# Taking 32 frames of the fifth dense tile out of the dense expert stage and gathering their expert rows instead

## The chip, the cores and the metric

The kernel runs on one core of one Trainium2 chip. The metric is the device time of one execution in microseconds (us), the median of three runs. The core has five engines that run their own instruction streams in order: TensorE (PE, with its weight loads PEld), VectorE (DVE), ScalarE (ACT), GpSimd (POOL) and SyncE (SP), which issues most transfers. The 16 DMA engines move data between HBM and on-chip memory.

## The reference, cut to what matters

One step of a one-layer encoder for 1024 new frames (8 tiles of 128) and 32 frames of a running stream ("S"). Attention and a recurrence come first. The change is in the expert layer behind them:

```
q  = (xs @ w_q)                        # per frame 8 heads x 2 queries
s  = scores against 128 + 128 keys per head
e  = the 16 best pairs of keys         # 8 x 16 = 128 experts of 16384 for each frame
gate = softmax(their scores)
hid  = gelu(down[e] . xs)              # 128 numbers for each frame
out  = sum over the 128 of gate*hid*up[e]
y    = RMSNorm(h + out)
```

Each expert is a row of `down` (1024 values) and a row of `up` (1024 values).

## The kernel before, in words

There are two ways to compute the expert layer, and the kernel uses both at once.

**Dense.** Tiles 0 to 4 (`DENSE`) go through all 16384 experts. `scatter` first builds for each frame a 128 x 128 table of its gates: for four frames at a time ScalarE makes a one-hot of the first index (`ohA`), VectorE and GpSimd one of the second times the gate (`ohB`), TensorE multiplies the two (`ws`), ScalarE copies the product into `stg`, and for every 16 frames (a group, `SB`) `stg` goes out to the table `W_d` in HBM, 1 MB each. There is one `stg` buffer. `v_start` transposes the frames and computes the first six blocks of 128 experts (`GE`, tile `early`); `stage_v` goes over all 128 blocks: `hidden` multiplies the frames by `down` (24 matmuls for each of two column halves `CS`, `CHUNK` columns each), `gated` multiplies by the gates read back from `W_d` (tile `gw`, one for each half of the frames) and splits the result into two parts (`vwh`, `vwl`), and the products with `up` are added to `acc` by VectorE. A *step* below is one block of `hidden` and a quarter of `up`'s work for four blocks: 96 matmuls and four additions to `acc` (L1274). There are 128 steps; the first four write `acc` instead of adding, so 496 additions follow. The last four steps have no `hidden`. `residual` then transposes `acc` back, adds the residual `h1`, and the five tiles are normed and written.

**Rows.** The other tiles, in the order `ROWS`, gather the 128 rows that each frame needs: for each k one indirect DMA (L1044) brings 128 rows of 8 KB, VectorE reduces the first half against the frame (L1047), ScalarE applies Gelu and the gate (L1049, L1050) and VectorE adds the second half, scaled, to `xp` (L1031). Five row buffers go round (`RB`). The 32 frames of S lie four times over the 128 partitions, each copy with a quarter of the experts: 32 gathers, and at the end the four partial sums are added (L1066 to L1071).

**The order.** Five generators (`gemm`, `attn`, `routing`, `scatter`, `rows`) are advanced by a small planner: whichever has the least virtual time goes next, each yield adding a cost (a step yields `6 * KD * n / 2400`, a row twice `GC`). `rows` and `routing` are also held behind VectorE instructions of `gemm` in the dense stage (`PACED`, `AHEADS`). A scheduler then fixes each engine's order. `routing` computes each tile's experts and gates (`topk`); tiles 6 and 7 are routed during the dense stage. `rows` begins when its pool is open, at the end of the projections.

Of the kernel before, what the change touches and what calls it, by code (L numbers as in the profile page):

```python
# [7 lines left out]
F32 = mybir.dt.float32  # L8
# [21 lines left out]
CDG = [[0, 1, 2], [3, 4], [5, 6, 7, "S"]]  # L30

DENSE = [0, 1, 2, 3, 4]
ROWS = [5, 6, "S", 7]
RORDER = [0, 1, 2, 3, 4, 5, 6, 7, "S"]

DEFER = [6, 7]
# [23 lines left out]

def rows_of(t):
    return DEC if t == "S" else 128


@with_exitstack
def step_kernel(ctx, tc, x_prompt, x_sample, cache_kT, cache_v, state, norm1, w_in, lam_params,
# [851 lines left out]
    def topk(t):  # L918
# [9 lines left out]
        for h0 in range(0, PH, hg):  # L928
# [54 lines left out]
            V.tensor_copy(out=e3[:T, h0:h0 + hg], in_=ef[:T])  # L983
            HEADS[t] = h0 + hg
            yield 1.0
        if t == "S":

            es = pk.tile([128, 32], I32, name="es", tag="es")
            gs = pk.tile([128, 32], F32, name="gts", tag="gts")
            for g in range(4):  # L990
                SP.dma_start(out=es[g * 32:(g + 1) * 32], in_=ei[:32, g * 32:(g + 1) * 32])
                SP.dma_start(out=gs[g * 32:(g + 1) * 32], in_=gate[:32, g * 32:(g + 1) * 32])
            ei, gate = es, gs
        ROUTE[t] = ROUTING[t] = (gate, ei)
        yield 3.0


    def normed(pool, ht, fnb, t, sq):

        T = rows_of(t)  # L1000
        ss = pool.tile([128, 1], F32, name="ssf", tag="ssf", bufs=2)
        A.activation(sq[:T], ht[:T], AF.Square, accum_out=ss[:T])
        r = rstd_of(pool, ss, 1, D, T, tag="f")
        V.scalar_tensor_tensor(out=sq[:T], in0=ht[:T], scalar=r[:T], in1=fnb[:T],
                               op0=OP.mult, op1=OP.mult)
        SP.dma_start(out=y_sample if t == "S" else y_prompt[t * 128:t * 128 + 128, :], in_=sq[:T])

    def rows():

        for t in ROWS:  # L1010
            while t not in ROUTING or "gat" not in P:
                yield None
            gate, ei = ROUTING[t]
            T = rows_of(t)
            nk = 32 if t == "S" else 128
            gat = P["gat"]

            def wide(name):
                return gat.tile([128, 2 * D], F32, name=name, tag="row", bufs=RB)

            xt = gat.tile([128, D], F32, name="xg", tag="xg", bufs=1)
            for g in range(128 // T):
                SP.dma_start(out=xt[g * T:(g + 1) * T], in_=xn_d[t][:, :])
            hid = gat.tile([128, 128], F32, name="hid", tag="hid", bufs=1)
            acc = P["xgp"].tile([128, D], F32, name="xp", tag="xp")

            def add(k, row):
                if k == 0 and t == "S":
                    V.tensor_scalar(acc, row[:, D:], hid[:, 0:1], None, op0=OP.mult)
                else:  # L1030
                    V.scalar_tensor_tensor(out=acc, in0=row[:, D:], scalar=hid[:, k:k + 1],  # L1031
                                           in1=acc if k else first, op0=OP.mult, op1=OP.add)

            first = None
            if t != "S":
                first = wide("first")[:, 0:D]
                SP.dma_start(out=first, in_=h1_d[t][:, :])

            late = []
            for k in range(nk):  # L1040
                while t not in ROUTE and HEADS.get(t, 0) * 16 <= k:
                    yield None
                row = wide("row")
                G.indirect_dma_start(out=row, out_offset=None, in_=p_rows,  # L1044
                                     in_offset=bass.IndirectOffsetOnAxis(ap=ei[:, k:k + 1], axis=0))
                h = hid[:, k:k + 1]
                V.tensor_tensor_reduce(out=row[:, 0:D], in0=row[:, 0:D], in1=xt, scale=1.0, scalar=0.0,  # L1047
                                       op0=OP.mult, op1=OP.add, accum_out=h)
# [12 lines left out]
            ht = acc  # L1061
            if t == "S":

                ht = hw[:, 0:D]
                SP.dma_start(out=ht[:T], in_=h1_d[t][:, :])
# [6 lines left out]
            normed(gat, ht, fnb, t, sq)  # L1072
            yield 4.0


    NV = 128 * len(DENSE)
    SB = 16
    W_d = dram([128 // JB, 128, NV // SB, JB, SB], "W_d")

# [10 lines left out]
    def grid(t, s0, q, stg, am, bm):  # L1090
        ps = ws_bank()
        for u in range(4):
            PE.matmul(ps[:, u * 128:(u + 1) * 128], am[:, u], bm[:, u], start=True, stop=True)  # L1093
        A.activation(stg[:, :, :, q:q + 4],
                     ps.rearrange("p (t b j) -> p b j t", t=4, j=JB), AF.Copy)
        if q + 4 == SB:
            o = (128 * DENSE.index(t) + s0) // SB
            SP.dma_start(out=W_d[:, :, o].rearrange("b i j t -> i b j t"), in_=stg)

    def scatter():  # L1100

        late = None
        for t in [x for ts in CDG for x in ts if x in DENSE]:
# [13 lines left out]
            A.activation(tr[:, 0:3], ps.rearrange("p (a t) -> p a t", a=4)[:, 0:3], AF.Copy)  # L1117
            A.activation(tr[:, 3], ps[:, 0:128], AF.Copy, scale=-1.0)

            for s0 in range(0, 128, SB):  # L1120
                stg = sct.tile([128, 128 // JB, JB, SB], F32, name="stg", tag="stg", bufs=1)
                for q in range(0, SB, 4):
                    pool, bufs = (P["oh"], OHB) if "oh" in P else (sct, 2)
# [48 lines left out]
    def v_start():  # L1172


        VX["early"] = P["vk"].tile([128, KD, NV], F32, name="early", tag="acc")
        xh = VX["xh"] = P["vx"].tile([128, KD, NV], F32R, name="vxh")
        xl = VX["xl"] = P["vx"].tile([128, KD, NV], F32R, name="vxl")

        places = [(t, i) for t in range(len(DENSE)) for i in range(2)]
        half = len(places) // 2  # L1180
        xs = []
        for h in range(2):
            x = P["gw"].tile([128, half, 512], F32, name="vxs", tag="gw", bufs=2)
            for j, (t, i) in enumerate(places[h * half:(h + 1) * half]):
                SP.dma_start(out=x[:, j], in_=xn_d[DENSE[t]][:, i * 512:(i + 1) * 512])
                xs.append(x[:, j])
        for (t, i), x in zip(places, xs):
            transposed_half(gv_bank, x, 128, halves(xh)[i], halves(xl)[i], 128 * t)
            yield 1.0
        for e in range(GE):  # L1190
            hidden(e)
            yield 3 * KD * NV / 2400.

    def stage_v():
        n = NV
        with tc.tile_pool(name="v_wk", bufs=2) as wk:
# [32 lines left out]
            def residual(d0):  # L1229

                cs = slice(d0 * 128, d0 * 128 + 512)
                for i in range(len(DENSE)):
                    ps = gv_bank()
                    for d in range(4):
                        PE.transpose(ps[:, d * 128:(d + 1) * 128],
                                     acc[:, d0 + d, i * 128:(i + 1) * 128], ident)
                    V.tensor_add(ht[:, i, cs], ht[:, i, cs], ps)
                    A.activation(sq[:, i, cs], ht[:, i, cs], AF.Square,
                                 accum_out=s2[:, d0 // 4, i:i + 1])
                    G.tensor_tensor(out=ht[:, i, cs], in0=ht[:, i, cs], in1=fnb[:, cs], op=OP.mult)  # L1240

            for jb in range(NJ):
                if jb == NJ - 1:
                    ht = P["vx"].tile([128, len(DENSE), D], F32, name="ht", tag="vxh")
                    sq = P["vx"].tile([128, len(DENSE), D], F32, name="sq", tag="vxl")
                    fnb = P["gw"].tile([128, D], F32, name="fnb", tag="gw", bufs=2)
                    s2 = wk.tile([128, 2, len(DENSE)], F32, name="s2", tag="s2", bufs=1)
                    ss = wk.tile([128, len(DENSE)], F32, name="ss", tag="ss", bufs=1)
                    late = [(ht[:, i], h1_d[t][:, :]) for i, t in enumerate(DENSE)]
# [28 lines left out]

            r = rstd_of(wk, ss, len(DENSE), D, tag="v")
            for i, t in enumerate(DENSE):  # L1280
                V.tensor_scalar(sq[:, i], ht[:, i], r[:, i:i + 1], None, op0=OP.mult)
                SP.dma_start(out=y_prompt[t * 128:t * 128 + 128, :], in_=sq[:, i])
            yield 10.0

    STATE = set()
# [162 lines left out]
```

## Time and profile before

| | us |
|---|---|
| median of three runs (3594.76 to 3604.02) | 3603.99 |
| profiled execution | 3604.3 |
| its span, first to last instruction | 3602.5 |
| TensorE busy | 3259.8 (90%) |
| VectorE busy | 2834.6 (79%) |
| GpSimd busy | 2018.5 (56%) |
| ScalarE busy | 1614.2 (45%) |

Busy shares are means over stages that have different limits. A line of a list of groups gives line, engine, operation, tiles (out<-in), shapes and count, then busy us and mean ns of one, then the engine's idle time before them with what ended it. A matmul's shown duration contains time in which the next one already runs; the distance from start to start is its real cost. PEclk is the share of 2.4 GHz that TensorE's clock was granted. In a table by stretch the engines come in the order PE, PEld, DVE, ACT, POOL, each with its busy us and its instructions; then PEclk, the DMA engines' busy share and GB/s.

### The profile page before, as it was taken

The page shows a single profiled execution, that of the slowest core. Times are in us where ns is not written, and L with a number is a line of the kernel's source. Part 1 is how long each engine was busy: PE and PEld are TensorE (multiplying, and loading weights), DVE is VectorE, ACT ScalarE, POOL GpSimd, SP SyncE. Part 2 cuts the span into 40 slices and gives each one's busy share as a digit, 9 for nine tenths or more (in the row PEclk, how much of TensorE's full clock was granted, in tenths as well). Part 3 has the DMA queues.
Part 4 walks back from the last instruction along what each step waited for, and adds up shares of the span by engine and source line. Part 5 has one row for each costly group of instructions (what it writes and reads, how often), then busy time and mean ns, then how long its engine had stood idle before and what let it go on. Part 6 is the DMA issues. An engine that isn't in the chain of part 4 may idle for free.

```text
span 3602.5 us, 60487 instructions
## 1 busy us (share of the span) xinstructions
PE 3259.8 (90%) x21635; PEld 3135.7 (87%) x21635; DVE 2834.6 (79%) x6148; ACT 1614.2 (45%) x4034; POOL 2018.5 (56%) x1339
## 2 busy tenths in 40 slices
PE   7999899989988888774899888999999999999997
PEld 6989899877877887774899888999999999999997
DVE  3354468898678999988999999888888888788833
ACT  3544344456777747763333333333333333333322
POOL 2322224546334556565666569666766676677633
PEclk9999999999988999886999999999999999999999
DMA  4554364444565635489888778999889898999832
GB/s 163 167 159 149 109 206 167 158 138 149 173 191 161 227 123 153 139 321 343 307 318 323 299 269 312 356 338 359 314 324 355 300 355 324 346 336 351 298 109 94
DMA packets 357453, 881.01 MB, mean 245 GB/s; under 512 B 31008, under 2 KB 190240, under 8 KB 299808
## 3 DMA queue, kind: packets, MB, share of 16 engines
q1 hardware_dynamic: 297248, 440.91, 36.9%
q0 software_dynamic: 59904, 436.23, 31.8%
q8 instruction: 171, 2.80, 0.3%
q14 instruction: 130, 1.06, 0.1%
HBM read 784.47 MB, written 92.14 MB: 243 GB/s over the span
## 4 chain that ended last, share of the span: by engine, by line
PE 57%; DVE 28%; DMA 4%; issue 4%; ACT 3%; POOL 2%; SPq 0%; DVEq 0%; ACTq 0%; POOLq 0%
PE gv L261 12%; PE gv L262 11%; PE gv L263 11%; PE gm L261 6%; PE gm L263 6%; PE gm L262 6%; DVE row L1047 5%; DVE xp L1031 5%; DVE acc L1274 2%; DVE oh L967 2%; PE ws L1093 1%; DVE ohB L1132 1%; DVE ef L972 1%; PE gb L468 1%; DMA row<-in_p_rows_dram,ei 1%
## 5 line engine op out<-in xcount | busy, mean ns | idle before, releaser
L261 PE MATMUL gv<-vwh,uh 128*128 128x320 f32 x2048 | 648.3, 317 | 96.7 <-DVE acc L1274 63.9
L255 POOL TENSOR_TENSOR wl<-wr,wh 128x1024 fp32r<-128x1024 f32 x160 | 390.4, 2453 | 540.7 <-ACT wh L254 524.9
L261 PE MATMUL gv<-vxh,dh 128*128 128x320 f32 x2048 | 643.9, 315 | 21.7 <-DVE acc L1274 10.2
L1044 POOL DMA_INDIRECT row<-in_p_rows_dram,ei x384 | 514.3, 1339 | 259.1 <-DVE xp L1031 141.7
L263 PE MATMUL gv<-vxh,dl 128*128 128x320 f32 x2048 | 639.8, 313 | 8.7 <-POOL dl L255 8.7
L262 PE MATMUL gv<-vwl,uh 128*128 128x320 f32 x2048 | 640.8, 313 | 0.0
L262 PE MATMUL gv<-vxl,dh 128*128 128x320 f32 x2048 | 639.7, 313 | 0.0
L263 PE MATMUL gv<-vwh,ul 128*128 128x320 f32 x2048 | 638.3, 313 | 0.5 <-POOL ul L255 0.5
L1047 DVE CUSTOM_DVE_ANT_0 row<-row,xg 128x1024 f32<-128x1024 f32 x416 | 599.4, 1441 | 3.1 <-DMA row<-in_p_rows_dram,ei 2.1
L1031 DVE SCALAR_TENSOR_TENSOR xp<-row,hid,xp 128x1024 f32<-128x1024 f32 x412 | 528.4, 1283 | 78.8 <-ACT hid L1050 77.0
L261 PEld LDWEIGHTS gv<-vwh,uh 128*128 128x128 f32 x2048 | 391.9, 191 | 111.6 <-DVE acc L1274 76.7
L255 POOL TENSOR_TENSOR dl<-dr,dh 128x512 fp32r<-128x512 f32 x256 | 361.3, 1415 | 201.4 <-ACT dh L254 193.4
L255 POOL TENSOR_TENSOR ul<-ur,uh 128x512 fp32r<-128x512 f32 x256 | 368.0, 1438 | 181.6 <-ACT uh L254 162.3
L261 PEld LDWEIGHTS gv<-vxh,dh 128*128 128x128 f32 x2048 | 392.0, 191 | 28.2 <-DVE vwl L255 13.1
L263 PEld LDWEIGHTS gv<-vxh,dl 128*128 128x128 f32 x2048 | 391.5, 191 | 9.5 <-POOL dl L255 9.5
L262 PEld LDWEIGHTS gv<-vwl,uh 128*128 128x128 f32 x2048 | 392.5, 192 | 0.0
L263 PEld LDWEIGHTS gv<-vwh,ul 128*128 128x128 f32 x2048 | 391.5, 192 | 0.9 <-POOL ul L255 0.9
L262 PEld LDWEIGHTS gv<-vxl,dh 128*128 128x128 f32 x2048 | 392.1, 191 | 0.0
L1135 POOL TENSOR_TENSOR ohB<-ohB,tr 128x512 f32<-128x512 f32 x160 | 200.0, 1256 | 262.4 <-DVE ohB L1132 216.8
L1274 DVE TENSOR_TENSOR acc<-acc,gv 128x320 f32<-128x320 f32 x496 | 235.4, 479 | 93.5 <-PE gv L263 90.2
L1049 ACT ACTIVATE hid<-hid 128x1 f32<-128x1 f32 x416 | 82.9, 199 | 486.5 <-DVE hid L1047 482.1
L254 ACT ACTIVATE uh<-ur 128x512 fp32r<-128x512 f32 x256 | 161.2, 630 | 301.3 <-PE gv L262 209.3
(324 smaller groups left out, 7520.7 us busy)
## 6 DMA issues: line engine op xcount, KB each, us to landing
dr<-in_p_downT_dram SPq DMA_DIRECT2D x256, 256.0 KB
ur<-in_p_up_dram SPq DMA_DIRECT2D x256, 256.0 KB
wr<-in_w_in_dram SPq DMA_DIRECT2D x88, 512.0 KB
W_d<-stg SPq DMA_DIRECT2D x40, 1024.0 KB
gw<-W_d SPq DMA_DIRECT2D x32, 1280.0 KB
wr<-in_p_wq_dram SPq DMA_DIRECT2D x48, 512.0 KB
wr<-in_w_out_dram SPq DMA_DIRECT2D x24, 512.0 KB
wr<-in_w_a_dram SPq DMA_DIRECT2D x12, 512.0 KB
```

The costliest lines, as they stand in the source:

```text
L254: A.activation(h, src, AF.Copy)
L255: (lo_engine or G).tensor_tensor(out=l, in0=src, in1=h.bitcast(F32), op=OP.subtract)
L261: PE.matmul(out, lh, rh, start=(i == 0), stop=False)
L262: PE.matmul(out, lh, rl, start=False, stop=False)
L263: PE.matmul(out, ll, rh, start=False, stop=(i == n - 1))
L967: V.tensor_tensor(out=oh[:T], in0=cf[:T, h].unsqueeze(2).to_broadcast([T, 16, NCAND]), in1=iota_c[:T].unsqueeze(1).to_broadcast([T, 16, NC ...
L1031: V.scalar_tensor_tensor(out=acc, in0=row[:, D:], scalar=hid[:, k:k + 1], in1=acc if k else first, op0=OP.mult, op1=OP.add)
L1044: G.indirect_dma_start(out=row, out_offset=None, in_=p_rows, in_offset=bass.IndirectOffsetOnAxis(ap=ei[:, k:k + 1], axis=0))
L1047: V.tensor_tensor_reduce(out=row[:, 0:D], in0=row[:, 0:D], in1=xt, scale=1.0, scalar=0.0, op0=OP.mult, op1=OP.add, accum_out=h)
L1049: A.activation(h, h, AF.Gelu)
L1135: G.tensor_tensor(out=bm, in0=bm, op=OP.mult, in1=tr[:, 2, xs].unsqueeze(2).to_broadcast([128, 4, 128]))
L1274: V.tensor_add(acc[:, db, cs], acc[:, db, cs], ps[:, :CHUNK])
```

## The change

Of tile 4 only the first 96 frames stay dense (`CUT`); the frames of the dense stage go from 640 to 608, so that every dense instruction that was 320 columns wide is 304 wide, the table `W_d` gets 38 groups instead of 40, and the yields become smaller in proportion. The other 32 frames become a new entry "4b" at the head of `ROWS`, treated as S is: four copies over the partitions, 32 gathers. Its experts and gates are cut out of those of tile 4 by eight small DMAs (L998, L999). The number of dense matmuls does not change.

```diff
-ROWS = [5, 6, "S", 7]
+CUT = {4: 96}
+ROWS = ["4b", 5, 6, "S", 7]
...
+def dense_of(t):
+    return CUT.get(t, 128)
...
-        if t == "S":
-            es = pk.tile([128, 32], I32, name="es", tag="es")
-            gs = pk.tile([128, 32], F32, name="gts", tag="gts")
+        if t == "S" or t in CUT:
+            es = pk.tile([128, 32], I32, name="es", tag="es", bufs=2)
+            gs = pk.tile([128, 32], F32, name="gts", tag="gts", bufs=2)
+            o = CUT.get(t, 0)
             for g in range(4):
-                SP.dma_start(out=es[g * 32:(g + 1) * 32], in_=ei[:32, g * 32:(g + 1) * 32])
-                SP.dma_start(out=gs[g * 32:(g + 1) * 32], in_=gate[:32, g * 32:(g + 1) * 32])
-            ei, gate = es, gs
-        ROUTE[t] = ROUTING[t] = (gate, ei)
+                SP.dma_start(out=es[g * 32:(g + 1) * 32], in_=ei[o:o + 32, g * 32:(g + 1) * 32])
+                SP.dma_start(out=gs[g * 32:(g + 1) * 32], in_=gate[o:o + 32, g * 32:(g + 1) * 32])
+            small = "%sb" % t if t in CUT else t
+            ROUTE[small] = ROUTING[small] = (gs, es)
+        if t != "S":
+            ROUTE[t] = ROUTING[t] = (gate, ei)
...
+            small = t in ("S", "4b")
+            T, of, o = (DEC, 4, CUT[4]) if t == "4b" else (rows_of(t), t, 0)
+            nk = 32 if small else 128
+            dst = y_sample if t == "S" else y_prompt[of * 128 + o:of * 128 + o + T, :]
...
-    NV = 128 * len(DENSE)
+    VT = [dense_of(t) for t in DENSE]
+    VO = [sum(VT[:i]) for i in range(len(VT))]
+    NV = sum(VT)
...
-            for s0 in range(0, 128, SB):
+            for s0 in range(0, dense_of(t), SB):
...
+                    V.memset(s2, 1.0)
...
             for i, t in enumerate(DENSE):
-                V.tensor_scalar(sq[:, i], ht[:, i], r[:, i:i + 1], None, op0=OP.mult)
-                SP.dma_start(out=y_prompt[t * 128:t * 128 + 128, :], in_=sq[:, i])
+                T = VT[i]
+                V.tensor_scalar(sq[:T, i], ht[:T, i], r[:T, i:i + 1], None, op0=OP.mult)
+                SP.dma_start(out=y_prompt[t * 128:t * 128 + T, :], in_=sq[:T, i])
```

The engines' orders are the same in both programs until shortly before the dense stage; from there the planner places things otherwise. Two places matter. The first is SyncE's queue just before the second half of the gate table is read back for the first block (`gw<-W_d`); `dr` and `ur` are loads of `down` and `up`. Before:

```order
L1098 DMA W_d<-stg 128x16x128
L1158 DMA dr<-in_p_downT_dram 128x512 x4
L1098 DMA W_d<-stg 128x16x128
L1158 DMA dr<-in_p_downT_dram 128x512 x5
L1098 DMA W_d<-stg 128x16x128
L1158 DMA dr<-in_p_downT_dram 128x512 x2
L1098 DMA W_d<-stg 128x16x128 x2
L1206 DMA gw<-W_d 128x2560
L1262 DMA ur<-in_p_up_dram 128x512 x6
```

And after:

```order
L1112 DMA W_d<-stg 128x16x128
L1172 DMA dr<-in_p_downT_dram 128x512 x2
L940 DMA scl<-sc_110 128x256
L1172 DMA dr<-in_p_downT_dram 128x512
L1112 DMA W_d<-stg 128x16x128
L1172 DMA dr<-in_p_downT_dram 128x512 x5
L1112 DMA W_d<-stg 128x16x128
L1172 DMA dr<-in_p_downT_dram 128x512 x2
L1220 DMA gw<-W_d 128x2432
L1276 DMA ur<-in_p_up_dram 128x512 x3
```

Ahead of this read the program has 40 writes of `W_d` before and 38 after. The last two before stand next to each other behind the last loads `dr`; after, the last write stands ahead of these loads.

The second place is the end of VectorE's program (`acc`: the dense sums; `ht`, `ss`, `sq`: the norm of the dense tiles; `row`, `xp`: reduction and addition of a gathered row of tile 7). Before:

```order
L1237 TENSOR_TENSOR ht<-ht,gv 128x512
L1274 TENSOR_TENSOR acc<-acc,gv 128x320 x2
L1237 TENSOR_TENSOR ht<-ht,gv 128x512 x4
L1274 TENSOR_TENSOR acc<-acc,gv 128x320 x4
L1237 TENSOR_TENSOR ht<-ht,gv 128x512 x5
L1277 TENSOR_TENSOR ss<-s_37996 128x5
L238 TENSOR_SCALAR msv<-ss 128x5
```

And after:

```order
L1296 TENSOR_SCALAR sq<-ht,rsv 128x1024 x3
L1059 ISA row,hid<-row,xg 128x1024
L1059 ISA hid 128x1
L1296 TENSOR_SCALAR sq<-ht,rsv 128x1024
L1043 SCALAR_TENSOR_TENSOR xp<-row,hid,xp 128x1024
L1296 TENSOR_SCALAR sq<-ht,rsv 96x1024
L1059 ISA row,hid<-row,xg 128x1024
L1059 ISA hid 128x1
L1043 SCALAR_TENSOR_TENSOR xp<-row,hid,xp 128x1024
L1059 ISA row,hid<-row,xg 128x1024
L1059 ISA hid 128x1
L1043 SCALAR_TENSOR_TENSOR xp<-row,hid,xp 128x1024
```

Before, the last row of tile 7 stands 52 additions ahead of the last one to `acc`. After, 27 reductions of tile 7 stand behind the last addition, 17 of them behind the last `sq`, most of them each directly ahead of its own addition to `xp`.

## Rows read from the trace of the kernel before

**Rows 1.** Busy time by stretch: window and length, then each engine, PEclk, DMA share, GB/s

```profile
1527.00:1678.00 151.00, 84.09 (x501) 80.50 (x499) 125.80 (x204) 79.21 (x223) 93.41 (x69) 0.74 0.92 338
1678.20:1741.90 63.70, 56.65 (x365) 55.46 (x366) 62.79 (x180) 27.76 (x76) 42.27 (x30) 0.95 0.84 316
1741.90:2282.60 540.70, 482.30 (x3059) 473.38 (x3058) 529.25 (x1088) 185.69 (x493) 380.20 (x265) 0.93 0.83 307
2282.60:3445.70 1163.10, 1139.53 (x7682) 1129.34 (x7681) 959.21 (x1461) 432.79 (x1165) 795.06 (x575) 1.00 0.89 331
3445.70:3582.00 136.30, 135.14 (x927) 134.61 (x926) 39.62 (x82) 35.51 (x73) 50.56 (x40) 1.00 0.25 81
3554.50:3582.00 27.50, 27.50 (x196) 27.50 (x195) 10.71 (x21) 7.08 (x16) 14.15 (x11) 1.00 0.12 38
3582.00:3602.50 20.50, 1.72 (x16) 1.49 (x14) 11.72 (x24) 3.17 (x10) 6.16 (x5) 0.59 0.32 128
```

**Rows 2.** Timeline of SyncE, writes of the gate table: start, length, instruction

```profile
1518.67 0.38 SPq L1098 DMA_DIRECT2D W_d<-stg  x1
...
1533.57 0.39 SPq L1098 DMA_DIRECT2D W_d<-stg  x1
...
1561.97 0.37 SPq L1098 DMA_DIRECT2D W_d<-stg  x1
...
1613.36 0.38 SPq L1098 DMA_DIRECT2D W_d<-stg  x1
...
1630.70 22.42 SPq L1098 DMA_DIRECT2D W_d<-stg  x2
```

**Rows 3.** Timeline of VectorE, gathered rows ahead of the dense stage

```profile
1657.15 1.22 DVE L1047 CUSTOM_DVE_ANT_0 row<-row,xg 128x1024 f32<-128x1024 f32 x1
...
1658.98 1.29 DVE L1031 SCALAR_TENSOR_TENSOR xp<-row,hid,xp 128x1024 f32<-128x1024 f32 x1 [0.60 <-ACT hid L1050]
1660.17 1.22 DVE L1047 CUSTOM_DVE_ANT_0 row<-row,xg 128x1024 f32<-128x1024 f32 x1
```

**Rows 4.** Timeline of VectorE, the first products with the gates

```profile
1678.15 3.58 DVE L1211 TENSOR_TENSOR early<-early,gw 128x320 f32<-128x320 f32 x6
```

**Rows 5.** Timeline of VectorE, end of S (L1066 to L1071)

```profile
2851.54 1.22 DVE L1066 COPY fnb<-xp 128x1024 f32<-128x1024 f32 x1
...
2864.31 1.69 DVE L1071 TENSOR_TENSOR ht<-ht,runs 32x1024 f32<-32x1024 f32 x1
```

**Rows 6.** Groups of VectorE, 1741.9 to 2282.6 us

```profile
L1047 DVE CUSTOM_DVE_ANT_0 row<-row,xg 128x1024 f32<-128x1024 f32 x111 | 176.1, 1587 | 1.9 <-DMA row<-in_p_rows_dram,ei 1.9
...
L1274 DVE TENSOR_TENSOR acc<-acc,gv 128x320 f32<-128x320 f32 x129 | 60.0, 472 | 2.6 <-PE gv L263 2.6
```

**Rows 7.** Groups of VectorE, 1640 to 1677 us

```profile
L1047 DVE CUSTOM_DVE_ANT_0 row<-row,xg 128x1024 f32<-128x1024 f32 x11 | 13.3, 1218 | 0.0
```

**Rows 8.** Timeline of TensorE, 39 matmuls of 320 columns apart

```profile
2504.73 0.31 PE L261 MATMUL gv<-vxh,dh 128*128 128x320 f32 x1
...
2510.45 0.31 PE L261 MATMUL gv<-vxh,dh 128*128 128x320 f32 x1
```

**Rows 9.** Timeline of TensorE, 19 matmuls of 256 columns apart

```profile
60.09 0.28 PE L262 MATMUL gm<-wl,xh 128*128 128x256 f32 x1
...
62.37 0.28 PE L263 MATMUL gm<-wh,xl 128*128 128x256 f32 x1
```

**Rows 10.** Timeline of VectorE, end of tile 7 and of the dense tiles

```profile
3423.13 1.29 DVE L1031 SCALAR_TENSOR_TENSOR xp<-row,hid,xp 128x1024 f32<-128x1024 f32 x1 [0.60 <-ACT hid L1050]
...
3430.56 1.27 DVE L1004 SCALAR_TENSOR_TENSOR ht<-xp,rsf,fnb 128x1024 f32<-128x1024 f32 x1
...
3583.00 3.08 DVE L1237 TENSOR_TENSOR ht<-ht,gv 128x512 f32<-128x512 f32 x5 [0.93 <-PE gv L1235]
...
3592.62 3.40 DVE L1281 TENSOR_SCALAR sq<-ht,rsv 128x1024 f32<-128x1024 f32 x5
```

**Rows 11.** Timeline of SyncE, the last writes

```profile
3593.43 4.14 SPq L1282 DMA_DIRECT2D out_dram<-sq  x5
```

More of the change, by code (lines that the diff above doesn't have):

```diff
@@ L985, in topk, with normed @@
             yield 1.0
-        if t == "S":
-            es = pk.tile([128, 32], I32, name="es", tag="es")
-            gs = pk.tile([128, 32], F32, name="gts", tag="gts")
+        if t == "S" or t in CUT:
+            es = pk.tile([128, 32], I32, name="es", tag="es", bufs=2)
+            gs = pk.tile([128, 32], F32, name="gts", tag="gts", bufs=2)
+            o = CUT.get(t, 0)
             for g in range(4):
-                SP.dma_start(out=es[g * 32:(g + 1) * 32], in_=ei[:32, g * 32:(g + 1) * 32])
-                SP.dma_start(out=gs[g * 32:(g + 1) * 32], in_=gate[:32, g * 32:(g + 1) * 32])
-            ei, gate = es, gs
-        ROUTE[t] = ROUTING[t] = (gate, ei)
+                SP.dma_start(out=es[g * 32:(g + 1) * 32], in_=ei[o:o + 32, g * 32:(g + 1) * 32])
[4 more added lines that the diff above has]
+            ROUTE[t] = ROUTING[t] = (gate, ei)
         yield 3.0
-    def normed(pool, ht, fnb, t, sq):
-        T = rows_of(t)
+    def normed(pool, ht, fnb, dst, sq):
+        T = dst.shape[0]
         ss = pool.tile([128, 1], F32, name="ssf", tag="ssf", bufs=2)
@@ L1005, in normed @@
                                op0=OP.mult, op1=OP.mult)
-        SP.dma_start(out=y_sample if t == "S" else y_prompt[t * 128:t * 128 + 128, :], in_=sq[:T])
+        SP.dma_start(out=dst, in_=sq[:T])
     def rows():
@@ L1022, in rows @@
             for g in range(128 // T):
-                SP.dma_start(out=xt[g * T:(g + 1) * T], in_=xn_d[t][:, :])
+                SP.dma_start(out=xt[g * T:(g + 1) * T], in_=xn_d[of][o:o + T, :])
             hid = gat.tile([128, 128], F32, name="hid", tag="hid", bufs=1)
@@ L1027, in add @@
             def add(k, row):
-                if k == 0 and t == "S":
+                if k == 0 and small:
                     V.tensor_scalar(acc, row[:, D:], hid[:, 0:1], None, op0=OP.mult)
@@ L1034, in rows @@
             first = None
-            if t != "S":
+            if not small:
                 first = wide("first")[:, 0:D]
@@ L1061, in rows @@
             ht = acc
-            if t == "S":
+            if small:
                 ht = hw[:, 0:D]
-                SP.dma_start(out=ht[:T], in_=h1_d[t][:, :])
+                SP.dma_start(out=ht[:T], in_=h1_d[of][o:o + T, :])
                 V.tensor_copy(out=full, in_=acc)
@@ L1071, in rows @@
                     V.tensor_add(ht[:T], ht[:T], part[:T])
-            normed(gat, ht, fnb, t, sq)
+            normed(gat, ht, fnb, dst, sq)
             yield 4.0
-    NV = 128 * len(DENSE)
+    VT = [dense_of(t) for t in DENSE]
+    VO = [sum(VT[:i]) for i in range(len(VT))]
+    NV = sum(VT)
     SB = 16
@@ L1096, in grid @@
         if q + 4 == SB:
-            o = (128 * DENSE.index(t) + s0) // SB
+            o = (VO[DENSE.index(t)] + s0) // SB
             SP.dma_start(out=W_d[:, :, o].rearrange("b i j t -> i b j t"), in_=stg)
@@ L1184, in v_start @@
             for j, (t, i) in enumerate(places[h * half:(h + 1) * half]):
-                SP.dma_start(out=x[:, j], in_=xn_d[DENSE[t]][:, i * 512:(i + 1) * 512])
+                SP.dma_start(out=x[:VT[t], j], in_=xn_d[DENSE[t]][:VT[t], i * 512:(i + 1) * 512])
                 xs.append(x[:, j])
         for (t, i), x in zip(places, xs):
-            transposed_half(gv_bank, x, 128, halves(xh)[i], halves(xl)[i], 128 * t)
+            transposed_half(gv_bank, x, VT[t], halves(xh)[i], halves(xl)[i], VO[t])
             yield 1.0
@@ L1231, in residual @@
                 cs = slice(d0 * 128, d0 * 128 + 512)
-                for i in range(len(DENSE)):
+                for i, (o, T) in enumerate(zip(VO, VT)):
                     ps = gv_bank()
                     for d in range(4):
[L1235 to L1240, printed above, removed]
+                        PE.transpose(ps[:T, d * 128:(d + 1) * 128], acc[:, d0 + d, o:o + T], ident)
+                    V.tensor_add(ht[:T, i, cs], ht[:T, i, cs], ps[:T])
+                    A.activation(sq[:T, i, cs], ht[:T, i, cs], AF.Square,
+                                 accum_out=s2[:T, d0 // 4, i:i + 1])
+                    G.tensor_tensor(out=ht[:T, i, cs], in0=ht[:T, i, cs], in1=fnb[:T, cs], op=OP.mult)
             for jb in range(NJ):
@@ L1248, in stage_v @@
                     ss = wk.tile([128, len(DENSE)], F32, name="ss", tag="ss", bufs=1)
-                    late = [(ht[:, i], h1_d[t][:, :]) for i, t in enumerate(DENSE)]
+                    V.memset(s2, 1.0)
+                    late = [(ht[:VT[i], i], h1_d[t][:VT[i], :]) for i, t in enumerate(DENSE)]
                     late.append((fnb, row_bcast(final_norm)))
```

2 lines of the change are left out of this document (removed).

## The prediction, made before the change was run

> **What bounds the kernel now.** I read the table by stretch first, since the busy shares of the page are means over stages with different limits [rows 1]. From 2282.6 to 3582.0 us TensorE is busy 98% at a granted clock of 1.00: whatever takes columns from its matmuls there moves the end. From 1678.2 to 2282.6 VectorE is busy 98 to 99% and TensorE 89%: there the time goes by VectorE's instructions, which are those of the gathered rows as much as the dense ones. From 1527.0 to 1678.0 TensorE is busy only 56% and VectorE 83%: the dense stage can't start until the table of gates is complete. The timeline of SyncE shows that: the last two of the 40 writes of `W_d` stand in one row from 1630.70, ending at 1653.1 [rows 2], and VectorE's first products with the gates read back begin at 1678.15 [rows 4]. Behind the dense stage nothing but the norm of the five tiles is left: the last product of the experts is added just before 3582.0, and the span ends 20.5 us later [rows 1]. Tile 7's rows are done long before, at 3423.13 + 1.29 [rows 10].
>
> The sum is made against the profiled execution, 3602.5 us of span and 1.8 us around it, 3604.3; the median shown is 3603.99, so no correction is needed.
>
> **Part by part.** Five terms, one for each stretch.
>
> *The table, two groups shorter.* The dense stage starts a fixed way behind the last write. Before, the 38th write issues at 1613.36 and the 40th at the end of its row, about 1652.7 [rows 2]: 39 us, of which I take −38. The loads of the frames and of the next blocks, which lay beside, don't hold the start: they precede the last writes in the queue. Bounds: two groups at the pace 1518.67 to 1533.57, −30; two at the pace 1533.57 to 1561.97, −57 [rows 2].
>
> *Start of the dense stage to the first addition.* Added here is the end of "4b", as S has it: a copy of 1.22 us, four additions of 32x1024 at 1.2 to 1.7, thirteen small instructions of the norm and a last product of about 1.3 [rows 5], some +10. Gone are three gathered rows, at 1.22 and 1.29 us busy with a wait of 0.60 between them 3.02 each [rows 3], −8 to −9. Taken: +2. The additions wait for three small transfers on VectorE, behind which the early products then stand, and eight small transfers go into SyncE's queue; bounds −8 and +15.
>
> *Addition 1 to 129, VectorE's stretch.* Two rows fewer, at 1.587 + 1.29 us [rows 6, 3], −6; the end of tile 5 moves behind addition 129 (one norm of 128x1024), −5; and the dense instructions shrink by 5%: 129 additions at 472 ns [rows 6] and as many others like them, by nothing at the least and 24 ns at the most, −3. Sum −14; bounds −5 (TensorE takes the place, with its gain only) and −25.
>
> *Addition 129 to 449, TensorE's stretch.* These 320 additions are 80 steps of 96 matmuls. A matmul of 320 columns costs (2510.45 − 2504.73)/39 = 146.7 ns [rows 8], one of 256 columns (62.37 − 60.09)/19 = 120.0 [rows 9]; 304 columns lie between at 140.0, which saves 6.67 ns each: 80 x 96 x 6.67 ns = 51 us. TensorE is busy 98% of it [rows 1], so −49 is taken. VectorE, at 82%, has 245 rows instead of 259 here, and isn't in the way. Bound on the other side −17: a third of it, if another engine sets the step. The upper bound of the saving is −51.
>
> *Behind addition 449.* Before: 136.3 + 20.5 = 156.8 us [rows 1]. Here the planner has put what it saved: of tile 7's rows 61 reductions now stand behind this point. The first 32 additions (108.8 us, the 136.3 less the 27.5 of the last stretch of the rows) shrink to 108.8 x 140.0/146.7 = 104; their 24 rows, at 1.22 + 1.19 us of VectorE each (the addition by its distance to the next start, 1658.98 to 1660.17, [rows 3]) 58, and some 60 dense instructions of about 0.5, fit under that. The last 16 additions have hardly any matmuls to hide behind: 10 rows at 3.02, 16 additions at 0.40 and five of the `ht` additions at 0.62 (3.08/5, rows 10) make 40, instead of 27.5. Behind the last addition stand 27 rows: ten have dense work between reduction and addition, so that the wait for ScalarE is filled, 10 x 2.42 + 3.1 (`ht`) + 3.4 (`sq`, [rows 10]) + 4 of small instructions = 35; seventeen stand each directly ahead of their own addition, 17 x 3.02 = 51. The end of the tile follows as tile 7's did: from the end of the last row's addition, 3424.4, to the end of the last product, 3431.8, 7.4 [rows 10]; then the transfer out, about 6, as from the last `sq` (it ends at 3596.0) to the end of the span [rows 10, 11, 1]. Sum 104 + 40 + 86 + 7 + 6 = 243, which is +86. The five buffers in turn cover the gathers, which have the DMA engines nearly for themselves. Bounds: +74 (the ten rows in the last 16 additions are hidden after all) and +98 (the last 27 rows at the 1.587 us of [rows 6], +10, and small waits for the gathers).
>
> In [rows 6] a reduction takes 1587 ns while GpSimd is busy 70% of the time with splitting weights; where it does nothing but issue gathers it takes 1218 [rows 7]. I take the latter for the end. The Trainium skill ("SBUF — State Buffer", Who interferes with whom) says that a VectorE instruction with two inputs in SBUF contends with a GpSimd instruction that reads SBUF; the two rows agree with it (the reduction is a custom instruction, which the page doesn't list). By that rule the last rows, with the splitting over, keep 1.22; at the longer duration the sum would be 10 us higher.
>
> Total: −38 + 2 − 14 − 49 + 86 = −13, 3604.3 − 13 = 3591.
>
> **The rivals.**
>
> *The table was later than its pace.* The last two groups may save two slow ones, as 1533.57 to 1561.97 [rows 2], for −57, and the rows between the last additions may be hidden, +74: −57 + 2 − 14 − 49 + 74 = −44, 3560. For it: VectorE is busy 83% ahead of the stage [rows 1] and has 13 rows fewer there. Against it: two thirds of these would have to be on the path. Chance 0.19.
>
> *All is given back.* The table saves only the quick pace, −30, and the last rows cost what they cost in [rows 6], +96: −30 + 2 − 14 − 49 + 96 = +5, 3609. For it: the last group before is slowed by gathered rows, which are still there. Chance 0.14.
>
> *TensorE's clock falls in the last steps.* In the last 16 additions TensorE waits for VectorE, 13 of 40 us. Where it had next to nothing to do, from 3582.0 on, it was granted 0.59, a mean between its levels of 1.2 and 2.4 GHz [rows 1]. If it falls to 1.2, the 26 us of matmuls take 52 instead of being covered by the 40: +12 to +14, 3604. The Trainium skill ("TensorE: Matmul & The Clock Gate", What's actually happening) says that the throttled clock is the default and that activity releases it. No row shows these steps with pauses of that size. Chance 0.07.
>
> *The step doesn't shrink: slower.* Between additions 129 and 449 a step takes (3445.7 − 2282.6)/80 = 14.54 us, of which 96 x 146.7 ns = 14.08 are matmuls. If what sets it is not the columns but the weights split by GpSimd and ScalarE, the gathers or VectorE, the step stays near 14.3 and only −17 remains, while the rows at the end are longer, since less is done beside: −38 + 2 − 14 − 17 + 92 = +25, 3629. It decides as soon as the step is above about 14.15 us: then the stretch gives less than 80 x 0.39 = 31, and the total passes +11. For it: DMA is busy 89% there and GpSimd 68% [rows 1], and neither shrinks by more than the gates' share. Against it: TensorE's 98%. Chance 0.18.
>
> **How the numbers follow.** The forecast has 0.42, with a range of its own from its bounds, 3574 to 3608: about 0.24 of it below 3593.2, 0.16 within and 0.02 above 3614.8. These two are 0.3% below and above the median, about what a measurement of this kernel can tell from no change. The first rival adds 0.19 to faster, the second and the third 0.21 to the same, the last 0.18 to slower: faster 0.43, same 0.37, slower 0.20. The range from 3558 to 3630 leaves out about a tenth on each side.
>
> **What would show it.** In the changed trace: the last write of `W_d` issues near 1613 and the first addition comes some 36 us earlier than before; between additions 1 and 129 VectorE is still at 98%; matmuls of 304 columns follow each other at 140 ns, and 80 steps take about 1114 us; from addition 449 to the last one 144 us pass, with TensorE waiting for VectorE in the last sixteen; then 27 reductions come at 2.4 to 3.0 us, the last 17 with a wait of 0.60 for ScalarE in each, and the span ends with a transfer of tile 7. The prediction is wrong if the table's last write stays near 1650, if the steps stay above 14.2 us, or if the last 27 rows wait for gathers.

## The result, and the profile after

The changed kernel takes 3564.6 us (median of 4 runs, 3559.5 to 3566.9) where the kernel before took 3604.0 beside it: a ratio of 0.9894, 95% interval 0.9876 to 0.9911, 39 us less. It was forecast at 3591, in a range of 3558 to 3630. The profiled execution spans 3563.3 us, 39.2 less than before, and that is what the stretches explain.

Each stretch runs between the starts of two additions to `acc` (the 1st, the 129th, the 449th, the 481st, the last); the last column is from there to the end of the span. The kernels of the experiments stand below the two. The changed kernel, run again, differs from itself by 4 to 5 us in each of the first two columns, so a difference of that size between two kernels shows nothing there.

| kernel | 1st at | 1 to 129 | 129 to 449 | 449 to 481 | 481 to last | last to end | span | rows behind the last addition |
|---|---|---|---|---|---|---|---|---|
| before | 1741.9 | 540.7 | 1163.1 | 108.8 | 27.1 | 20.9 | 3602.5 | 0 |
| changed | 1704.5 | 506.2 | 1106.4 | 106.2 | 45.1 | 94.9 | 3563.3 | 27 |
| changed, run again | 1709.1 | 502.2 | 1106.6 | 106.3 | 45.6 | 95.1 | 3564.9 | 27 |
| no 4b | 1710.5 | 517.6 | 1105.8 | 106.9 | 33.7 | 20.0 | 3494.5 | 0 |
| table of 40 groups | 1741.3 | 511.6 | 1116.7 | 106.9 | 44.8 | 86.0 | 3607.3 | 23 |
| columns 320 | 1711.4 | 531.2 | 1157.2 | 111.9 | 48.3 | 27.1 | 3587.1 | 3 |
| addition behind the next reduction | 1702.1 | 501.5 | 1105.0 | 107.2 | 39.7 | 106.3 | 3561.8 | 29 |
| four row buffers | 1691.9 | 523.9 | 1104.7 | 106.1 | 41.0 | 135.0 | 3602.6 | 39 |
| 112 frames dense | 1702.4 | 520.0 | 1136.7 | 108.1 | 47.7 | 36.4 | 3551.3 | 6 |
| 64 frames dense | 1665.6 | 517.2 | 1058.4 | 107.0 | 46.7 | 279.9 | 3674.8 | 95 |

The busy time by stretch of the changed kernel, in the columns of [rows 1]:

```profile
1704.50:2210.70 506.20, 457.13 (x3090) 447.70 (x3089) 502.64 (x1059) 183.53 (x484) 383.37 (x261) 0.95 0.86 318
2210.70:3317.10 1106.40, 1078.96 (x7653) 1070.01 (x7652) 927.09 (x1420) 417.11 (x1135) 759.08 (x564) 1.00 0.91 336
3317.10:3423.30 106.20, 104.01 (x741) 103.08 (x740) 91.82 (x137) 39.32 (x107) 70.98 (x54) 1.00 0.89 326
3423.30:3468.80 45.50, 29.21 (x195) 27.38 (x193) 36.84 (x51) 11.73 (x36) 28.48 (x21) 0.89 0.74 267
3468.80:3563.30 94.50, 0.55 (x3) 0.29 (x3) 80.38 (x119) 17.82 (x66) 45.15 (x29) 0.51 0.79 314
```

Read from left to right in each line: in the first two stretches the same engines are full as before, VectorE (502.6 of 506.2) and TensorE (1079.0 of 1106.4). The last line is new: 94.5 us in which TensorE does nothing and VectorE is busy 85%, with rows of tile 7. Before, 20.9 us stood there.

The writes of the gate table on SyncE's timeline (start, length), which answer to [rows 2] (`stg`, the one buffer for a group):

```profile
1503.40 0.37 SPq L1112 DMA_DIRECT2D W_d<-stg  x1
1518.25 0.38 SPq L1112 DMA_DIRECT2D W_d<-stg  x1
1532.91 0.38 SPq L1112 DMA_DIRECT2D W_d<-stg  x1
...
1556.75 0.37 SPq L1112 DMA_DIRECT2D W_d<-stg  x1
1581.14 0.38 SPq L1112 DMA_DIRECT2D W_d<-stg  x1
1602.81 0.69 SPq L1112 DMA_DIRECT2D W_d<-stg  x1
```

The 38th and last write issues at 1602.8, 50 us ahead of the 40th before. Up to the 35th the two kernels agree within a microsecond (1532.9 and 1533.6); the three behind it come 23 us apart, before 27.

Two matmuls of 304 columns, 42 apart on TensorE's timeline, beside [rows 8, 9]:

```profile
2503.69 0.30 PE L267 MATMUL gv<-vxh,dh 128*128 128x304 f32 x1
...
2509.55 0.30 PE L267 MATMUL gv<-vxh,dh 128*128 128x304 f32 x1
```

(2509.55 − 2503.69)/42 = 139.5 ns. The reductions of VectorE's stretch, in the list of groups from 1704.5 to 2210.7, against [rows 6]:

```profile
L1059 DVE CUSTOM_DVE_ANT_0 row<-row,xg 128x1024 f32<-128x1024 f32 x109 | 164.8, 1512 | 0.0
L1288 DVE TENSOR_TENSOR acc<-acc,gv 128x304 f32<-128x304 f32 x128 | 56.9, 452 | 0.0
```

Two reductions fewer, and each 75 ns shorter. And VectorE's timeline where the last rows stand alone, against [rows 3]:

```profile
3517.63 1.22 DVE L1059 CUSTOM_DVE_ANT_0 row<-row,xg 128x1024 f32<-128x1024 f32 x1
3518.77 0.08 DVE L1059 DVE_READ_ACCUMULATOR2_ANT hid<- 128x1 f32 x1
3519.45 1.29 DVE L1043 SCALAR_TENSOR_TENSOR xp<-row,hid,xp 128x1024 f32<-128x1024 f32 x1 [0.60 <-ACT hid L1062]
3520.65 1.22 DVE L1059 CUSTOM_DVE_ANT_0 row<-row,xg 128x1024 f32<-128x1024 f32 x1
```

It is the loop of [rows 3] again, 3.02 us for a row, with the 0.60 us in which ScalarE makes the scale. VectorE's order puts nothing else into that time.

### The profile page after: what moved, and what is told of

It is laid out like the page before. It is cut to its first block, busy times and chain, and to the rows that moved or that the text cites. A ratio compares the mean times of both kernels' runs of the same rounds, so it can differ in the third digit from the quotient of the medians.

```text
span 3563.3 us, 60542 instructions
## 1 busy us (share of the span) xinstructions
PE 3161.3 (89%) x21571; PEld 3034.4 (85%) x21571; DVE 2905.1 (82%) x6255; ACT 1605.4 (45%) x4052; POOL 2046.4 (57%) x1363
## 4 chain that ended last, share of the span: by engine, by line
PE 53%; DVE 33%; issue 5%; DMA 4%; ACT 3%; POOL 2%; SPq 0%; ACTq 0%; POOLq 0%; DVEq 0%
PE gv L267 10%; PE gv L268 10%; PE gv L269 10%; DVE xp L1043 6%; PE gm L267 6%; PE gm L269 6%; PE gm L268 5%; DVE row L1059 5%; DVE ohB L1146 2%; DVE oh L973 2%; DVE acc L1288 2%; DVE ef L978 1%; PE ws L1107 1%; PE gb L474 1%; POOL oh L976 1%
## 5 line engine op out<-in xcount | busy, mean ns | idle before, releaser
L267 PE MATMUL gv<-vwh,uh 128*128 128x304 f32 x2048 | 631.6, 309 | 89.5 <-DVE acc L1288 52.8
L1059 DVE CUSTOM_DVE_ANT_0 row<-row,xg 128x1024 f32<-128x1024 f32 x448 | 656.8, 1467 | 2.6 <-DMA row<-in_p_rows_dram,ei 2.6
L267 PE MATMUL gv<-vxh,dh 128*128 128x304 f32 x2048 | 630.9, 308 | 27.6 <-DVE acc L1288 10.8
L1043 DVE SCALAR_TENSOR_TENSOR xp<-row,hid,xp 128x1024 f32<-128x1024 f32 x443 | 568.1, 1282 | 107.2 <-ACT hid L1062 105.9
L269 PE MATMUL gv<-vxh,dl 128*128 128x304 f32 x2048 | 621.8, 305 | 4.4 <-POOL dl L261 4.2
L268 PE MATMUL gv<-vxl,dh 128*128 128x304 f32 x2048 | 625.4, 306 | 0.0
L268 PE MATMUL gv<-vwl,uh 128*128 128x304 f32 x2048 | 624.0, 305 | 1.1 <-DVE vwl L261 1.1
L269 PE MATMUL gv<-vwh,ul 128*128 128x304 f32 x2048 | 618.9, 305 | 4.6 <-POOL ul L261 4.6
L1149 POOL TENSOR_TENSOR ohB<-ohB,tr 128x512 f32<-128x512 f32 x152 | 188.1, 1243 | 258.1 <-DVE ohB L1146 220.5
L1288 DVE TENSOR_TENSOR acc<-acc,gv 128x304 f32<-128x304 f32 x496 | 226.5, 461 | 42.9 <-PE gv L269 41.2
```

Of the source, the lines that this page charges most:

```text
L267: PE.matmul(out, lh, rh, start=(i == 0), stop=False)
L268: PE.matmul(out, lh, rl, start=False, stop=False)
L269: PE.matmul(out, ll, rh, start=False, stop=(i == n - 1))
L1149: G.tensor_tensor(out=bm, in0=bm, op=OP.mult, in1=tr[:, 2, xs].unsqueeze(2).to_broadcast([128, 4, 128]))
L1288: V.tensor_add(acc[:, db, cs], acc[:, db, cs], ps[:, :CHUNK])
```

## The experiments

Theory: the change removes two things from the path of the dense stage, the two groups of the table ahead of it and 5% of its matmuls' columns, and pays with gathered rows that no longer fit beside it and stand behind its end. The rivals give each part another worth. The first three runs take one part away each, the next two ask what sets the pace of the last rows, and the last ones change the number of frames.

**Without the rows of 4b.**

```diff
-ROWS = ["4b", 5, 6, "S", 7]
+ROWS = [5, 6, "S", 7]
```

> The changed kernel without the 32 gathered rows of 4b: its 32 frames are left out of the output; table, dense width and all else as in the changed kernel. Theory: the 32 gathers are paid for at the end, as rows of tile 7 that no longer fit beside the dense stage. In this order no row stands behind the last addition to acc and 3 stand in the last 16. So from addition 449 to the end 104 + 28 + 21 = 153 us instead of 246, and 4b's ending (some 10 us) is gone ahead of the first addition: about 3465 us. Rival: the rows of 4b cost what they cost where they stand, ahead of the dense stage, where VectorE has room: then only the 10 to 15 us there go, 3550.

Measured: 3493.0 us, 0.9686 of before (0.9662 to 0.9710), 72 us less than the changed kernel. Its last stretch by busy time:

```profile
3474.50:3494.50 20.00, 1.41 (x13) 1.15 (x11) 12.12 (x24) 3.17 (x10) 6.16 (x5) 0.67 0.33 125
```

The 75 us behind the last addition are gone, as the theory has it; the 32 gathers, which stand first in `ROWS`, are paid for at the end by other rows, so the rival falls. The time is 28 us above the 3465 expected. Of it 27 lie ahead of addition 449, which was to come 10 us earlier than in the changed kernel and comes 17 later: the first addition is 6 us later (hardly more than the changed kernel differs from itself), and the stretch 1 to 129 is 11 longer, with VectorE idle 17.4 us in it instead of 3.6 and with the end of tile 5 (6.5 us of its norm) back in it.

**The table of 40 groups kept.**

```diff
-    W_d = dram([128 // JB, 128, NV // SB, JB, SB], "W_d")
+    W_d = dram([128 // JB, 128, NV // SB + 2, JB, SB], "W_d")
...
-            for s0 in range(0, dense_of(t), SB):
+            for s0 in range(0, 128, SB):
```

> The changed kernel, but the table of gates is built for all 128 frames of tile 4: 40 groups written as before the change, the last two read by nobody. Theory: the two groups are on the path to the dense stage: last write of W_d near 1650 instead of 1603, first addition to acc at about 1745 (+40). But 8 more rows run in that time (41 instead of 33 before the first addition) and 23 instead of 27 stand behind the last addition, which gives 12 to 24 us back: 3581 to 3592 us. Rival: the gathered rows alone set the end, the table only shifts dense work beside them: 3565 to 3570.

Measured: 3607.7 us, 1.0002 of before (0.9987 to 1.0018): with this part undone nothing of the gain is left. SyncE's timeline, the last four writes:

```profile
1583.11 0.38 SPq L1112 DMA_DIRECT2D W_d<-stg  x1
1606.83 0.58 SPq L1112 DMA_DIRECT2D W_d<-stg  x1
...
1630.10 27.40 SPq L1112 DMA_DIRECT2D W_d<-stg  x2
```

From the 38th write to the 40th (at the end of the last row, 1657.1) pass 50 us, and the first addition is at 1741.3, 36.8 later than in the changed kernel: the groups were on the path, at nearly the size forecast. They were not on it by the read-back, though, which in this run takes the first 38 groups only. VectorE's products with the gates begin 16 us ahead of the last write; then VectorE waits for ScalarE:

```profile
1640.68 2.41 DVE L1225 TENSOR_TENSOR early<-early,gw 128x304 f32<-128x304 f32 x6
1657.30 1.29 DVE L1043 SCALAR_TENSOR_TENSOR xp<-row,hid,xp 128x1024 f32<-128x1024 f32 x1 [10.05 <-ACT hid L1062]
```

and ScalarE, which makes the scale of a row behind the copy of the last group in its own order, for the one `stg`:

```profile
1651.96 1.09 ACT L1108 ACTIVATE stg<-ws 128x512 f32<-128x512 f32 x2 [7.16 <-DMA W_d<-stg]
```

What the theory had wrong is the repayment. Only 9 us come back at the end (86.0 instead of 94.9), and the stretches between take 16 more; in the second of them 11 us of VectorE's routing work stand that were done ahead of addition 129 in the changed kernel.

**Matmuls 320 columns wide again.**

```diff
+    WIDE = CHUNK + 16
+    WS = [(slice(0, WIDE), slice(0, CHUNK)), (slice(NV - WIDE, NV), slice(16, WIDE))]
...
-            mm3(ps[:, :CHUNK], [(dn[k], (VX["xh"][:, k, cs], VX["xl"][:, k, cs])) for k in range(KD)])
+            mm3(ps[:, :WIDE], [(dn[k], (VX["xh"][:, k, mc], VX["xl"][:, k, mc])) for k in range(KD)])
```

(the same for the products with `up`; what reads `ps` takes the 304 columns that it owns)

> The changed kernel with every dense matmul 320 columns wide again (the two column halves overlap by 32 columns, of which nothing is used); table, gates, VectorE's and ScalarE's shapes stay at 304. Theory: 12288 matmuls cost 7.2 ns more each, 55 us of it between additions 129 and 449 and some 20 elsewhere; but the rows go on beside it, 3 instead of 27 stand behind the last addition to acc, and 24 x 3.0 = 72 us go at the end: 3560 to 3575 us, no difference that could be told, though the last addition comes some 75 us later (near 3543). Rival: the columns are the gain itself: 3564 + 75 = 3640. Second rival: the step was never set by columns: the last addition stays near 3468 and the end falls.

Measured: 3589.1 us, 0.9954 of before (0.9938 to 0.9970), 24 above the changed kernel. By stretch:

```profile
2242.60:3399.80 1157.20, 1134.79 (x7682) 1126.06 (x7681) 954.36 (x1465) 429.25 (x1168) 797.59 (x582) 1.00 0.90 337
3399.80:3560.00 160.20, 142.35 (x937) 139.54 (x935) 130.39 (x194) 50.86 (x145) 101.20 (x76) 0.95 0.85 311
3560.00:3587.10 27.10, 0.55 (x3) 0.30 (x3) 20.39 (x49) 6.38 (x20) 9.43 (x5) 0.54 0.41 155
```

Neither the theory nor its rivals hit it. The end is shorter by 68 us, as said; but the last addition comes 92 us later, not 75: besides 51 between additions 129 and 449 (7680 matmuls, 55 expected) 25 come in the stretch that VectorE sets, where 114 rows now stand instead of 109 (probably because the scheduler's model sees a longer matmul, which was not tested). The other 16 come before the first addition and behind the 449th. So in these two orders the narrower columns are worth 92 us of dense time and cost 68 us of rows that they uncover: 24.

**The wait for ScalarE taken out of the last rows.** Each of the last additions of tile 7 is queued behind the next row's reduction.

```diff
+                red = [i for i in nc.cur_bb.bb.instructions[-4:] if i.engine == V.engine][-1]
...
-                    add(*late.pop(0))
+                    with tc.issue_after(red) if t == 7 and k >= 88 else nullcontext():
+                        add(*late.pop(0))
```

> The changed kernel with one edge more: for the last 40 rows of tile 7 each addition to xp is queued behind the reduction of the next row, so that VectorE has work while ScalarE makes the scale. Theory: the 0.60 us waits in the last rows are VectorE's own: 17 x 0.60 = 10 us less, 3554 us. Rival: the gathers take their place at once (one row is 1.05 MB, 2.75 us of the 16 DMA engines by the share of their queue): 17 x (3.02 - 2.75) = 5 us, 3560. Second rival: nothing at all, since the rows arrive only every 3.0 us: 3564.

Measured: 3568.1 us, 0.9903 of before (0.9876 to 0.9930): no difference from the changed kernel. VectorE's waits from the last `sq` to the end (us, times, longest us), first of the changed kernel:

```profile
DVE xp L1043 <- ACT hid L1062: 6.0, 10, 0.6
DVE row L1059 <- DMA row<-in_p_rows_dram,ei: 2.1, 1, 2.1
DVE msf L244 <- ACT ht L1011: 1.2, 1, 1.2
```

and of this one:

```profile
DVE row L1059 <- DMA row<-in_p_rows_dram,ei: 11.1, 8, 2.7
DVE msf L244 <- ACT ht L1011: 1.2, 1, 1.2
```

The wait for ScalarE is gone and one for the gathers stands in its place, 11.1 instead of 8.1 us in all; two more reductions also fell behind the last addition. The second rival's time came out, by the first rival's mechanism: from 3501.5 on sixteen rows come 2.99 us apart on the mean, and from 3500 to 3545 the DMA engines are busy 99%. The rows can't come much faster than they are asked for now.

**Four row buffers.** Is it the number of buffers that sets the pace of the last rows?

```diff
-RB, VR, VB, BB, OHB = 5, 3, 2, 4, 4
+RB, VR, VB, BB, OHB = 4, 3, 2, 4, 4
```

> The changed kernel with four row buffers instead of five. Theory: the last rows follow a round of the buffers: an addition frees one, GpSimd issues the next gather, some 12 us later it lands. With five buffers and 3.0 us for a row that just fits; with four the rows come every 12 to 14.5 us / 4 = 3.0 to 3.6 us and VectorE waits for gathers in nearly each of them; in this order 39 instead of 27 reductions stand behind the last addition, so the end is 12 x 3.0 + 39 x 0.5 = 45 to 55 us later: 3610 to 3620. Rival: VectorE and its wait for ScalarE set the pace at 3.02 whatever the buffers: only the 12 rows more, 3600.

Measured (one run): 3604.4 us, 39 above the 3565.2 that the changed kernel took beside it. VectorE's waits from 3500 us to the end:

```profile
DVE xp L1043 <- ACT hid L1062: 10.2, 17, 0.6
DVE row L1059 <- DMA row<-in_p_rows_dram,ei: 8.1, 5, 3.1
DVE msf L244 <- ACT ht L1011: 1.2, 1, 1.2
```

The rival is right. 39 reductions stand behind the last addition instead of 27, and the stretch is 40 us longer: 12 x 3.0 = 36 and some waits for gathers. The last rows alone are not the whole difference, though: the first addition is 13 us earlier and the stretch 1 to 129 is 18 longer. With four buffers most rows still follow each other at 3.02 us. The pace of the last rows is VectorE's with its wait for ScalarE; the gathers come just behind it, and only when that wait is taken out do they show.

**Half the change, and twice.** If dense time and rows trade against each other, 32 frames need not be the best number. With 112 frames dense, 16 are gathered, in eight copies; the halves of the columns are 320 and 304. With 64 dense, two entries of 32 are gathered.

```diff
-CUT = {4: 96}
+CUT = {4: 112}
...
+            w = 128 - o if o else DEC
+            for g in range(128 // w):
+                SP.dma_start(out=es[g * w:(g + 1) * w, :w], in_=ei[o:o + w, g * w:(g + 1) * w])
...
-    CS = [slice(j * CHUNK, (j + 1) * CHUNK) for j in range(NCH)]
+    GH = [-(-(NV // SB) // 2), NV // SB // 2]
+    CS = [slice(0, GH[0] * SB), slice(GH[0] * SB, NV)]
```

> Half the change: 112 frames of tile 4 stay dense (column halves of 320 and 304), 16 frames are gathered, eight copies over the partitions, 16 gathers; the table has 39 groups. In this order 6 reductions stand behind the last addition to acc instead of 27. Theory: dense time and rows trade against each other: the start and the stretches 1 to 449 lose half of what the change gave (table +20, columns +28 and +5), the last addition comes at about 3523; the end behind it is as in the kernel with 320 columns (27 us with 3 rows) plus 3 rows: 36; 3560 us of span, as the whole change (3563): no difference that can be told. Rival: the rows behind the end are pure loss: 21 fewer rows at 3.0 us are 63 us, and only the table's 20 us are given back: 3520. Second rival: half the gain, 3585.

```diff
-CUT = {4: 96}
-ROWS = ["4b", 5, 6, "S", 7]
+CUT = {4: 64}
+SMALL = {"4b": (4, 64), "4c": (4, 96)}
+ROWS = ["4b", "4c", 5, 6, "S", 7]
```

> The change done twice: 64 frames of tile 4 stay dense, two entries of 32 frames each are gathered (64 gathers), 36 groups of the table, columns 288 wide. In this order 95 reductions stand behind the last addition instead of 27. Theory: the last addition comes about 115 us earlier (table 40, columns 55 to 80), near 3350, but 68 more rows at 3.0 us follow it: 3350 + 95 + 204 = 3650 us, slower than before the change. Rival: every 32 frames bring the same, 39 us: 3525.

The changed kernel ran beside them again:

> The changed kernel once more, on the same chip as the half change, so that the two can be compared: 3559 to 3568 us.

Measured: 112 frames 3552.2 us, 0.9852 of before (0.9828 to 0.9875); 96 frames 3565.2, 0.9887 (0.9871 to 0.9904); 64 frames 3678.1, 1.0201 (1.0180 to 1.0221). The stretch behind the last addition, with 112 frames dense:

```profile
3514.90:3551.30 36.40, 0.55 (x3) 0.30 (x3) 30.11 (x57) 7.39 (x24) 12.40 (x8) 0.55 0.61 231
```

and with 64:

```profile
3394.90:3674.80 279.90, 0.55 (x3) 0.28 (x3) 243.68 (x325) 52.13 (x204) 145.46 (x97) 0.50 0.92 360
```

Half the change beats both kernels by its median, 13 us below the whole change. The intervals still touch, but the four runs of the one (3544.5 to 3560.9) all lie below the four of the other (3563.4 to 3568.3). Its end of 36.4 us is as expected; the surprise is the start: with 39 groups the first addition is at 1702.4, no later than with 38, although the last write goes out 15 us later, at 1617.5. Between that write and the first addition 14 reductions stand instead of 18. The first addition is 22 us ahead of where the expectation has it (20 behind the changed kernel's), and 11 of these are lost again up to addition 449; that is also why "no difference" was too high. Twice the change is far on the other side, its rival is out by 150 us, and its theory by 25 (3674.8 us of span against 3650): 74 us of dense time are gained where 115 were expected, and 68 more rows cost 185, at 2.7 us each, with the DMA engines busy 92% of the stretch. So by the medians 32 frames are already past the best point of the three tried, and the last rows are what decides it.

## Why the prediction was right, and where its sizes were off

The direction and each of the five stretches came out with the sign forecast, but the gain is three times the 13 us. By the table above, measured against forecast:

- **Start of the dense stage** (the first two terms together): −37.4 against −36. Singly they were off and cancel, so that the sum is right by luck. The last write came 50 us earlier, not 38. The two groups took 39 before, as read from the trace; the other 10 us are the three writes ahead of them, which went out 23 us apart in the changed kernel instead of 27. The table of 40 groups takes 50 for the same two. The second term was +12.5 against +2: the norm of 4b took 10.8 us of VectorE, as worked out, but routing work moved up into this stretch (+5) and VectorE waited 5 us more. What was wrong behind both is that the stage "starts a fixed way behind the last write". From the last write to the first addition pass 89.2 us before, 101.7 in the changed kernel, 107.3 without 4b (its norm is gone, and six more additions to `xp` stand there), 84.1 with the table of 40 groups and 84.9 with 112 frames. VectorE is idle for at most 13 of these us in any kernel: the way is as long as the work of VectorE that the planner puts there. VectorE waits for the read-back in one run only, 3.3 us with 112 frames; with the table of 40 groups it is ScalarE and its one `stg` through which the table holds the stage.
- **Addition 1 to 129: −34.5 against −14, the step that was mis-sized.** It had counted instructions and, but for the dense ones, left their durations. VectorE's time in the stretch by kind, from start to start: reductions −11.0 (two fewer are 3 of it, the rest is 73 ns on each), additions to `xp` −4.5 (four fewer), dense instructions −5.7 against −3, the end of tile 5 −3.7 against −5, routing −1.8, and idle time −7.8, which the sum did not have at all. The 73 ns are collisions with GpSimd (below): 65 of the 109 reductions overlapped its tensor work and took 1.72 us on the mean, before 69 of 111 and 1.82. Why they cost less isn't settled: GpSimd was busy 76% of the stretch, before 70%. (The prediction put these 70% down to the splitting of weights; of the 380 us that is 186, and 153 are issues of gathers, beside which no reduction was held up.) Other kernels vary here as much, from 501 to 531 us, with 103 to 114 rows in the stretch (95 with 64 frames dense), and the time does not follow the rows alone.
- **Addition 129 to 449: −56.7 against −49.** The columns were the cause, as said; the term was sized by a straight line between 256 and 320 columns, 140.0 ns, and by a cut to −49. The matmuls follow at 139.4 on the mean where 320 columns take 146.6; 7680 times the 7.2 ns are 55 us. The run with 320 columns takes 51 of these back.
- **Behind addition 449: +89.4 against +86.** 106.2, 45.1 and 94.9 us against 104, 40 and 99. The errors of the last two cancel. In the last 16 additions TensorE was to wait for VectorE. Its longest wait is another: for ScalarE's `uh`, which waits for a load of `up` (`ur`) while the DMA engines are busy throughout (3423.3 to 3439.0). VectorE, too, stands behind ScalarE there, and later one of its reductions lasts 4.30 us beside GpSimd's products:

```profile
3438.55 0.63 ACT L260 ACTIVATE uh<-ur 128x512 fp32r<-128x512 f32 x1 [7.13 <-DMA ur<-in_p_up_dram]
3439.23 0.62 PE L267 MATMUL gv<-vwh,uh 128*128 128x304 f32 x1 [10.03 <-ACT uh L260]
3439.63 1.29 DVE L1043 SCALAR_TENSOR_TENSOR xp<-row,hid,xp 128x1024 f32<-128x1024 f32 x1 [5.76 <-ACT hid L1062]
3457.03 4.30 DVE L1059 CUSTOM_DVE_ANT_0 row<-row,xg 128x1024 f32<-128x1024 f32 x1
```

Behind the last addition the rows cost what was summed, 35.6 us up to the last `sq` and 50.6 for the seventeen rows behind it, against 35 and 51; the end of the tile and the transfer took 8.7 instead of 13.

Of the rivals, the first (3560) came nearest in time, and for half of its reason: the table gave 50 of its 57 us, though not by the last two groups alone. The rows in the last 16 additions were not hidden, though. The second (3609) is out: the start gave 37 and not 28, and the end cost 89 and not 96. The rival with the step that doesn't shrink is out: a step takes 13.83 us. The clock's rival happened in small, and not behind a wait for VectorE: in and after TensorE's pause of 10 us for `uh` the granted clock was 0.50, the level of 1.2 GHz, from 3433.1 to 3443.3 (0.89 over the stretch). Most matmuls from 3439.2 to 3443.3 followed each other at 0.25 us instead of 0.14, which is some 2 us in all, an estimate from these rows, in a stretch of 45 us of which VectorE was busy 36.8.

The parts don't add: without the narrow table the kernel is as slow as before, without the narrow columns it is 24 us slower than with, and the rows alone cost 72. All three are differences from the changed kernel with the order planned anew each time, so a part's worth and the worth of its order are not told apart.

## What to carry to other kernels

When work is moved from a stage that one engine fills to a queue that runs beside it, count what that queue has left over until the stage ends: what doesn't fit stands alone behind it, at its full price, and the shorter stage uncovers still more of it (68 of the 92 us here). Then try a half and a double of the amount before arguing about the whole. And in a stretch that one engine fills, count the durations as well as the instructions: of the 20 us missed in that stretch, 8 were the same instruction running shorter and 8 were idle time.

## What the runs showed of the hardware

A gathered row's reduction on VectorE (two inputs in SBUF) is held up by GpSimd's tensor work and by nothing else seen here. In the changed kernel, between additions 1 and 129, 44 reductions beside nothing or beside the issue of a gather took 1.20 to 1.21 us on the mean, none over 1.4; the 65 that overlapped a tensor instruction of GpSimd took 1.64 and 2.03 us on the mean (52 that met the splitting of weights first, 13 that met routing's products first); before, the same two kinds took 1.66 and 2.38. One case on the timelines of VectorE:

```profile
3476.73 4.53 DVE L1059 CUSTOM_DVE_ANT_0 row<-row,xg 128x1024 f32<-128x1024 f32 x1
```

and GpSimd:

```profile
3476.48 3.70 POOL L1253 TENSOR_TENSOR ht<-ht,fnb 128x512 f32<-128x512 f32 x3
3480.34 1.78 POOL L1056 DMA_INDIRECT row<-in_p_rows_dram,ei  x1 [0.16 <-issue]
```

The reduction of 1.22 us lasts 4.53: GpSimd's three products end at 3480.18, and it ends 1.1 us behind them. That is the rule of the Trainium skill ("SBUF — State Buffer", Who interferes with whom), that a VectorE instruction with two inputs in SBUF contends with a GpSimd instruction that reads SBUF, here for a custom instruction that the page doesn't list. Also unexpected: a matmul of 304 columns costs 7.2 ns less than one of 320, and one of 288 (64 frames dense) 132.6 ns, again 6.8 less; the straight line between 256 and 320 columns gives 6.67 [rows 8, 9].
